# FFN-in of a hybrid conv block: product 1 of a third dual among the first products, and other pools for some of its banks

## The chip, the cores and the metric

One core of a Trainium2 chip runs the whole kernel. The metric is the time of one execution on the device in microseconds (us); the kernel before was run three times for it. Besides, one execution was profiled, and all single durations below are read from that one. TensorE (PE in the profile) does the matmuls, VectorE (DVE) and ScalarE (ACT) the elementwise work, GpSimd (POOL) some of it and part of the DMA issues, SyncE (SP) the loads of weights.

## The reference, cut to what matters

One layer of a streaming encoder: a mixing part, then a gated FFN, each behind an RMSNorm with a modulation from `c`. The change lies where the FFN begins.

```python
D_MODEL = 1024; SEQ = 1024; BATCH = 1; D_FF = 2816
...
mix = jnp.einsum('bsd,de->bse', g_a * y_a + g_b * y_b, w_o[l])
x = x + g1 * mix

h2 = rms_norm(x, norm_ffn_g[l]) * (1.0 + sc2) + sh2
a, bgate = jnp.split(jnp.einsum('bsd,df->bsf', h2, w_ffn_in[l]), 2, axis=-1)
x = x + g2 * jnp.einsum('bsf,fd->bsd', jax.nn.silu(a) * bgate, w_ffn_out[l])
...
return rms_norm(x, final_norm_g)
```

Everything is float32.

## The kernel before, in words

**Layout.** Activations lie with their channels on the 128 partitions: 8 blocks of channels by 1024 tokens, and the tokens are taken as two halves of 512, `halves[0]` and `halves[1]`. A PSUM bank holds 128 x 512 numbers, one output block for one half. A float32 operand is split into a high part, which the matmul takes as it is, and a low part, the rest: `wh` and `wl` for weights, names ending in `h` and `l` for activations. One step of a contraction is three matmuls, high by high, high by low and low by high (L283, L284, L286 in `mm3`).

**Duals.** The first matrix product of the FFN (FFN-in) has 22 blocks of 128 hidden channels, each for `a` and for `bgate`. The kernel takes two such blocks at a time, in 11 *duals*. A dual is a 2 x 2 block product: rows are `a` and `bgate`, the contraction of 1024 is two halves of 512, and columns are the two token halves. Strassen's scheme in Winograd's form does it with seven products of smaller matrices instead of eight. They are run in the order `PRODUCTS = "1265734"`. I write (d, m) for product m of dual d. One product is 24 matmuls: 2 hidden blocks (p = 0, 1), 4 contraction blocks, 3 matmuls each.

**Operands.** `ts[m]` holds the four activation pairs of product m. Products 1 and 2 need the normed `h2` of the first token half alone (pairs `h20` to `h27`). The others need combinations with the second half: t2 (product 6), t1 (5), t3 (7), b22 (3), t4 (4). So products 1 and 2 can run while the second half's norm is still being made. `norm_2_start` and `rstd_end` make `r2`, the reciprocal root of the second half's mean square (it begins at L338, with `r2t`). `norm_2_half(k, r2)` then makes h2 of the second half for channel blocks k and k + 4 (L824), and from it the t2 pair of k, whose low part is written by L323 after ScalarE's L322. `norm_2_last` makes the pairs of t1, t3, b22 and t4.

**Weights.** The left operands are sums of weight blocks. Raw blocks of 128 x 1024 numbers, 512 KB, are loaded by SyncE (L191) into five `raw` buffers. `dual_units` makes the weights of a product from them. For product 6 it adds three times (L228, L229, L230, called first, second and third sum below), for product 3 once (L232, the fourth sum); the result goes to product 6, 5, 7 or 3. `split_w` then writes `wh` on ScalarE (L205) and `wl` on VectorE (L206). Both have three buffers, and `next_w` prepares the weights two products ahead of the one about to run (`AHEAD = 2`). For a dual that is not `early`, product 1 loads all four blocks, 11, 12, 21 and 22, and the sums are in place. An `early` dual loads one block where product 1 and one where product 2 comes; the others are loaded only when products 6, 3 and 4 come, seven loads in all.

**Banks.** PSUM has eight banks: `ps` with six and `ps2` with two. A dual takes two banks of each of three kinds, for p = 0 and 1: x collects products 1, 6, 7 and 4 (each adds to what stands there), y takes product 2, z collects 5 and 3. `in_evac` reads a bank when a product of it is complete: copies for 1, 6 and 5 (L905, ScalarE), and additions on VectorE for 2 (L907), 7 (L910) and 3 (L914).

**Order.** A scheduling layer turns the program into one list of instructions for each engine, and each engine works its list in order. An instruction that waits holds all that stand behind it on its engine. The order of the products is written in `in_order`, and the weights are planned in the same order:

```python
in_order = [(d, m) for d in range(2) for m in "12"] + [(d, m) for d in range(2) for m in PRODUCTS[2:]]
in_order += [(d, m) for d in range(2, N_IN) for m in PRODUCTS]
```

So it begins (0,1), (0,2), (1,1), (1,2), then products 6, 5, 7, 3, 4 of duals 0 and 1. Ahead of it runs the last of the mixing part, `mix(j, h)`: it adds each block's result to `x` (L811), squares it on ScalarE and sums the squares (L819). The calls of `norm_2_half` stand between the first products. All this work for the second token half is on VectorE and ScalarE in the same 60 us in which TensorE runs the first products.

Of the kernel before, what the change touches and what calls it, by code (L numbers as in the profile page):

```python
# [91 lines left out]

PRODUCTS = "1265734"

GROUP, GROUPS = 3, 3
# [10 lines left out]
def block_kernel(ctx: ExitStack, tc: tile.TileContext, x0, xT, c, vecs, ada, w_first, w_plain, w_duals,  # L108
# [29 lines left out]
    def ps_tile(name):  # L138
        return psp.tile([P, H], F32, tag="ps", name=name)
# [4 lines left out]
    def hl_tile(name, dt=F32R):  # L144
        return tp.tile([P, H], dt, tag="t", name=name)
# [38 lines left out]
    def raw_tile(n=1024):  # L184

        raws.append(raws.pop(0))
        return raws[-1].tile([P, 1024], F32, tag="raw", name="raw")[:, :n]

    def load(src, n=1024):
        raw = raw_tile(n)  # L190
        nc.sync.dma_start(raw, src)  # L191
        return raw
# [6 lines left out]
    def split_w(raw, n, after=(), lo_engine=nc.vector):  # L199
        wh = whp.tile([P, 1024], F32R, tag="wh", name="wh")[:, :n]  # L200
        wl = wlp.tile([P, 1024], F32R, tag="wl", name="wl")[:, :n]
        with ExitStack() as order:
            for ins in after:
                order.enter_context(tc.issue_after(ins))
            nc.scalar.copy(wh, raw)  # L205
            lo = lo_engine.tensor_tensor(wl, raw, f32(wh), ALU.subtract)  # L206
        if n == T and lo_engine is nc.gpsimd:
            pool_los.append(lo.ins)
        return wh, wl

    def dual_units(mats, n, early=False, eng=nc.vector):

        a = {}

        def get(*blocks):
            for b in blocks:
                a[b] = load(mats[("11", "12", "21", "22").index(b)], n)

        def unit(m):
            if early:  # L220
                get(*{"1": ("11",), "2": ("12",), "6": ("21", "22", "11"), "3": ("12",), "4": ("22",)}.get(m, ()))
            elif m == "1":
                get("11", "12", "21", "22")
            if m in "12":
                return split_w(a["1" + m], n, (), eng)
            if m == "6":
                a["s1"] = a["22"] if early else raw_tile(n)
                eng.tensor_tensor(a["s1"], a["21"], a["22"], ALU.add)  # L228
                eng.tensor_tensor(a["21"], a["21"], a["11"], ALU.add)  # L229
                eng.tensor_tensor(a["11"], a["11"], a["s1"], ALU.add)  # L230
            elif m == "3":
                eng.tensor_tensor(a["12"], a["12"], a["11"], ALU.add)  # L232
            return split_w(a[{"6": "11", "5": "s1", "7": "21", "3": "12", "4": "22"}[m]], n, (), eng)

        return {m: (lambda m=m: unit(m)) for m in PRODUCTS}
# [11 lines left out]
    def next_w(ahead=AHEAD):  # L247

        fetch(ahead + 1)
        return ready.pop(0)  # L250
# [24 lines left out]
    def mm3(outs, wsl, w, xs, first, last, again=False):  # L275

        if w[1] is None:
            for ps, x in zip(outs, xs):
                mm3.ins = nc.tensor.matmul(ps, w[0][:, wsl], x, start=first, stop=last).ins
            return  # L280
        wh, wl = w[0][:, wsl], w[1][:, wsl]
        for ps, (xh, xl) in zip(outs, xs):
            nc.tensor.matmul(ps, wh, xh, start=first, stop=False, skip_group_check=again)  # L283
            nc.tensor.matmul(ps, wh, xl, start=False, stop=False, skip_group_check=again)  # L284
        for ps, (xh, _) in zip(outs, xs):
            mm3.ins = nc.tensor.matmul(ps, wl, xh, start=False, stop=last, skip_group_check=again).ins  # L286
# [5 lines left out]
            mm3(outs, slice(k * P, k * P + P), w, [act[k][h] for h in hs], k == 0, k == KC - 1)  # L292
        return outs

    def product(banks, m, t, evac=None, between=None, y_tile=ps2_tile):

        w = next_w()
        b = {"1": "x", "6": "x", "7": "x", "4": "x", "2": "y", "5": "z", "3": "z"}[m]
        n = len(t)
        for p in range(2):  # L300
            if m in "125":
                banks[b, p] = (y_tile if b == "y" else ps_tile)(b)
            ps = banks[b, p]
            for k in range(n):
                c0 = (p * n + k) * P
                mm3([ps], slice(c0, c0 + P), w, [t[k]], m in "125" and k == 0, k == n - 1, m in "6734")
            if evac:
                evac(p, m, ps)
            if between and p == 0:
                between()  # L310
# [7 lines left out]
    def t_pair(name):  # L318
        return hl_tile(name + "h"), hl_tile(name + "l")

    def t_split(src, hi, lo):
        nc.scalar.copy(hi, src)  # L322
        nc.vector.tensor_tensor(lo, src, f32(hi), ALU.subtract)  # L323

    def minus(out, a, b):

        nc.vector.scalar_tensor_tensor(out=out, in0=a, scalar=-1.0, in1=b, op0=ALU.mult, op1=ALU.subtract)
# [60 lines left out]
    x = {}  # L388
# [22 lines left out]
    def uc_tile(name, n=T + CK - 1, dt=F32):  # L411
        return ucp.tile([P, T + CK - 1], dt, tag="uc", name=name)[:, :n]
# [24 lines left out]
    for k in range(0, KC, 2):  # L437
        t = uc_tile("x0", T)
# [62 lines left out]
    KH = KC // 2  # L501
# [228 lines left out]
    banks = [[ps_tile(b) for _ in range(2)] for b in "xyz"]  # L730
# [90 lines left out]
    def h2_of(k, h, r2, hi_lo=None):  # L821

        t = x1[k][:, halves[h]]
        nc.vector.scalar_tensor_tensor(out=t, in0=t, scalar=aff2[:, k : k + 1], in1=r2, op0=ALU.mult, op1=ALU.mult)  # L824
        if hi_lo:
            hi, lo = hi_lo
            nc.scalar.activation(hi, t, AF.Identity, bias=modc(24 + k))
            nc.vector.scalar_tensor_tensor(
                out=lo, in0=t, scalar=modc(24 + k), in1=f32(hi), op0=ALU.add, op1=ALU.subtract
            )  # L830
        nc.scalar.activation(t, t, AF.Identity, bias=modc(24 + k))
        return t


    ts = {m: [None] * (KC // 2) for m in PRODUCTS}
# [9 lines left out]
    def norm_2_half(k, r2):  # L845

        h2_of(k, 1, r2)
        b22 = h2_of(k + KH, 1, r2)
        b11, b12 = (x1[k][:, s] for s in halves)
        nc.vector.tensor_tensor(b11, b11, b12, ALU.subtract)  # L850
        t2.append(hl_tile("t2", dt=F32))
        minus(t2[k], b11, b22)
        ts["6"][k] = t_pair("t2")
        t_split(t2[k], *ts["6"][k])
# [29 lines left out]


    N_IN = FC // 2
    in_units = [dual_units([w_fi[d, m] for m in range(4)], 1024, d < 2) for d in range(N_IN)]
    in_order = [(d, m) for d in range(2) for m in "12"] + [(d, m) for d in range(2) for m in PRODUCTS[2:]]
    in_order += [(d, m) for d in range(2, N_IN) for m in PRODUCTS]
    plan += [in_units[d][m] for d, m in in_order]  # L890
    ha = {}
    in_banks = [{} for _ in range(N_IN)]
# [7 lines left out]
    def in_evac(d):  # L900
        def evac(p, m, ps):
            f = 2 * d + p
            if m in "165":
                ha[f, m] = t = in_tile(d, m)
                nc.scalar.copy(t, ps)  # L905
            elif m == "2":
                nc.vector.tensor_tensor(ha[f, "1"], ps, ha[f, "1"], ALU.add)  # L907
            elif m == "7":
                t = ha[f, "5"]
                nc.vector.tensor_tensor(t, ps, t, ALU.add)  # L910
                nc.scalar.activation(t, t, AF.Silu, scale=-1.0)
            elif m == "3":
                t = ha[f, "6"]
                nc.vector.tensor_tensor(t, ps, t, ALU.add)  # L914
                nc.vector.tensor_tensor(t, t, ha[f, "5"], ALU.mult)
            else:
                t = gip.tile([P, H], F32, tag="g", name="g4")
                nc.scalar.activation(t, ps, AF.Silu, scale=-1.0)
                nc.vector.tensor_tensor(t, t, ha[f, "1"], ALU.mult)
                ha[f, "4"] = t  # L920
        return evac
# [39 lines left out]
    def group_load(g, m):  # L961
        to[g, m] = [t_load((g * GROUP + i, m)) for i in range(GROUP)]

    def in_product(d, m):
        product(in_banks[d], m, ts[m], in_evac(d), y_tile=ps_tile if d == 1 else ps2_tile)
        if d == N_IN - 1:
            group_load(0, m)

# [4 lines left out]
    r2 = None  # L973
    product(in_banks[0], "1", ts["1"], in_evac(0), norm_2_start)
    r2 = rstd_end(*r2)
    for i, (d, m) in enumerate(in_order[1:4]):
        norm_2_half(i, r2)
        in_product(d, m)
    norm_2_half(KH - 1, r2)
    norm_2_last()  # L980
    close(*phase_1)
    raws.append(open_pool("raw_a", 1, side="right", stack=ctx)[1])
    x1ap = open_pool("x1a", 2, side="right", stack=ctx)[1]
    phase_2 = [open_pool("gi", 7), open_pool("stage", 3, side="right")]
    gip, stagep = (p for _, p in phase_2)
    for d, m in in_order[4:]:
        in_product(d, m)
        if m == PRODUCTS[-1]:
            if 2 <= d < 6:
                for i in range(40 + 2 * (d - 2), 42 + 2 * (d - 2)):  # L990
                    modulation(i, x1ap.tile([P, T], F32, tag="x1", name="ada"))
            hid_set(d)
# [31 lines left out]
    for g in range(GROUPS):  # L1024
        for d in range(2):
            banks = {}
# [177 lines left out]
```

## Time and profile before

| | us |
|---|---|
| runs | 1502.62, 1504.49, 1505.2 (median 1504.49) |
| profiled execution, own time | 1502.96 |
| its span (first to last instruction) | 1501.2 |
| mean granted TensorE clock | 0.995 of full |
| loads of `in_w_fi` (weights of the FFN's first product) | 50 of 512 KB, 4.3 us from issue to landing in the median |

A row of the timeline has its start in the span, the time of one instruction, the engine, the line, the operation and its tiles; where the engine stood idle before it, the idle time and what ended it follow in brackets. A row of waits has the engine, line and tile that waited, the engine and tile that released it, the idle time, how often, and the longest. A window row gives each engine's busy time and number of instructions in a stretch, the clock granted to TensorE in it (PEclk), and the share of DMA bandwidth.

### The profile page before, as it was taken

To read this page: it belongs to the slowest core of one execution; us is meant where nothing else is said; L and a number is where in the kernel's file an instruction comes from. 1 tells how busy PE (TensorE), PEld (TensorE's weight loads), DVE (VectorE), ACT (ScalarE), POOL (GpSimd) and SP (SyncE) were. 2 spreads that over 40 slices of the span, in tenths; PEclk is the share of its full clock that TensorE was granted. 3 is DMA by queue.
4 is the path that set the end of the run, shared out by engine and by line. 5 is a ranking of instruction groups with operands and counts; after the bars stand their busy time and mean duration, and the time that the engine had idled before them with its cause. 6 is when DMAs were issued, how large, how long until landed. Compare 5 with 4: busy or idle time off the path is not lost.

```text
span 1501.2 us, 17711 instructions
## 1 busy us (share of the span) xinstructions
PE 1469.3 (98%) x6455; PEld 1202.0 (80%) x6455; DVE 1141.0 (76%) x1569; ACT 623.1 (42%) x896; POOL 538.2 (36%) x467
## 2 busy tenths in 40 slices
PE   6999999999999999999999989999999999999997
PEld 2788888888888788887788868888888888888887
DVE  7994999887887984777767789776666665667755
ACT  4653433443343353244345454444444443222235
POOL 0037777777767773410121001111000016444005
PEclk9999999999999999999999989999999999999999
DMA  9522223232222268555765337544444449998403
GB/s 352 207 64 74 94 71 112 70 108 75 98 71 85 99 261 299 167 175 175 231 207 183 126 98 236 200 169 153 152 149 150 153 148 351 364 324 256 141 28 112
DMA packets 82697, 247.24 MB, mean 165 GB/s; under 512 B 9521, under 2 KB 11697, under 8 KB 82610
## 3 DMA queue, kind: packets, MB, share of 16 engines
q1 hardware_dynamic: 41776, 137.91, 27.4%
q0 software_dynamic: 36944, 95.44, 19.2%
q10 hardware_dynamic: 3890, 12.78, 2.2%
q8 instruction: 50, 0.82, 0.2%
q14 instruction: 37, 0.30, 0.1%
HBM read 183.69 MB, written 62.39 MB: 164 GB/s over the span
## 4 chain that ended last, share of the span: by engine, by line
PE 93%; DVE 4%; issue 1%; ACT 1%; DMA 1%; POOL 0%; POOLq 0%; ACTq 0%; DVEq 0%
PE x L286 11%; PE x L284 11%; PE x L283 10%; PE z L283 7%; PE z L284 7%; PE z L286 7%; PE y L284 6%; PE y L283 6%; PE y L286 6%; PE ya L284 2%; PE mix L286 2%; PE mix L284 2%; PE ya L283 2%; PE ya L286 2%; PE mix L283 2%; PE yb L283 2%
## 5 line engine op out<-in xcount | busy, mean ns | idle before, releaser
L205 ACT CAST wh<-raw 128x1024 fp32r<-128x1024 f32 (+2 forms) x257 | 259.4, 1010 | 482.8 <-PE z L284 122.0
L206 POOL TENSOR_TENSOR wl<-raw,wh 128x1024 fp32r<-128x1024 f32 x92 | 227.2, 2471 | 131.1 <-ACT wh L205 130.9
L206 DVE TENSOR_TENSOR wl<-raw,wh 128x1024 fp32r<-128x1024 f32 (+2 forms) x165 | 188.4, 1142 | 52.7 <-ACT wh L205 50.0
L671 DVE SCALAR_TENSOR_TENSOR c<-diff,vec,c 128x512 f32<-128x512 f32 x248 | 178.6, 751 | 3.3
L930 POOL DMA_DIRECT2D hid<-stage x71 | 37.9, 534 | 358.7 <-DVE stage L323 353.0
L283 PE MATMUL x<-th,wh 128*128 128x512 f32 x240 | 93.4, 389 | 0.0
L284 PE MATMUL x<-tl,wh 128*128 128x512 f32 x240 | 93.4, 389 | 0.0
L286 PE MATMUL x<-th,wl 128*128 128x512 f32 x240 | 93.4, 389 | 0.0
L671 DVE SCALAR_TENSOR_TENSOR c<-u,wsum,c 128x512 f32<-128x512 f32 x112 | 84.1, 751 | 1.8
L264 DVE CUSTOM_DVE_ANT_0 raw<-raw,cs,vec 128x1024 f32<-128x1024 f32 x24 | 35.5, 1486 | 50.6 <-DMA raw<-in_ada 50.6
L283 PE MATMUL z<-th,wh 128*128 128x512 f32 x168 | 65.4, 389 | 0.0
L284 PE MATMUL z<-tl,wh 128*128 128x512 f32 x168 | 65.4, 389 | 0.0
L286 PE MATMUL z<-th,wl 128*128 128x512 f32 x168 | 65.4, 389 | 0.0
L228 POOL TENSOR_TENSOR raw<-raw 128x1024 f32<-128x1024 f32 x12 | 29.8, 2482 | 95.0 <-DVE wl L206 94.2
L322 ACT CAST stage<-g 128x512 fp32r<-128x512 f32 x62 | 38.3, 621 | 52.0 <-DMA hid<-stage 25.1
L323 DVE TENSOR_TENSOR stage<-g,stage 128x512 fp32r<-128x512 f32 x62 | 42.5, 688 | 20.5 <-ACT stage L322 20.4
L956 POOL DMA_DIRECT2D th<-hid x71 | 38.1, 537 | 52.0 <-PE x L286 28.3
L283 PE MATMUL yb<-zsh,wh 128*128 128x512 f32 x128 | 50.0, 391 | 2.8 <-DVE gb L793 2.8
L283 PE MATMUL x<-t2h,wh 128*128 128x512 f32 x120 | 47.7, 400 | 5.1 <-ACT wh L205 2.8
L286 PEld LDWEIGHTS x<-th,wl 128*128 128x128 f32 x240 | 45.1, 188 | 9.4
L283 PEld LDWEIGHTS x<-th,wh 128*128 128x128 f32 x240 | 45.1, 188 | 9.3
L284 PEld LDWEIGHTS x<-tl,wh 128*128 128x128 f32 x240 | 45.1, 188 | 9.3
(1012 smaller groups left out, 4263.8 us busy)
## 6 DMA issues: line engine op xcount, KB each, us to landing
hid<-stage POOLq DMA_DIRECT2D x71, 512.0 KB, 4.0
raw<-in_w_fi SPq DMA_DIRECT2D x50, 512.0 KB, 4.3
raw<-in_w_duals SPq DMA_DIRECT2D x48, 512.0 KB, 3.5
th<-hid POOLq DMA_DIRECT2D x71, 256.0 KB, 5.9
tl<-hid POOLq DMA_DIRECT2D x71, 256.0 KB, 6.0
ada<-in_ada SPq DMA_DIRECT2D x24, 512.0 KB, 5.8
raw<-in_ada SPq DMA_DIRECT2D x24, 512.0 KB, 4.5
raw<-in_w_fo SPq DMA_DIRECT2D x24, 384.0 KB, 6.2
```

The source lines that it names most:

```text
L205: nc.scalar.copy(wh, raw)
L206: lo = lo_engine.tensor_tensor(wl, raw, f32(wh), ALU.subtract)
L228: eng.tensor_tensor(a["s1"], a["21"], a["22"], ALU.add)
L264: nc.vector.tensor_tensor_reduce(out=raw, in0=raw, in1=cs, scale=1.0, scalar=col(V_ADA, b), op0=ALU.mult, op1=ALU.add, accum_out=modc(b),)
L283: nc.tensor.matmul(ps, wh, xh, start=first, stop=False, skip_group_check=again)
L284: nc.tensor.matmul(ps, wh, xl, start=False, stop=False, skip_group_check=again)
L286: mm3.ins = nc.tensor.matmul(ps, wl, xh, start=False, stop=last, skip_group_check=again).ins
L322: nc.scalar.copy(hi, src)
L323: nc.vector.tensor_tensor(lo, src, f32(hi), ALU.subtract)
L671: tap.ins = nc.vector.scalar_tensor_tensor(out=out, in0=src[:, s : s + H], scalar=wt, in1=acc, op0=ALU.mult, op1=ALU.add).ins
L930: nc.gpsimd.dma_start(hid_dram[key], s)
L956: nc.gpsimd.dma_start(t, hid_dram[key][:, s])
```

## The change

It sets `FRONT = 3`: the first products are now (0,1), (0,2), (1,1), (1,2) and (2,1). After them the order is as it was: products 6, 5, 7, 3 and 4 of duals 0 and 1, then the rest of dual 2. Dual 2 becomes `early`, so it loads seven blocks instead of four. The banks of (2,1) are not read when it is done, but right before (2,2), by the same copies (L905). So that banks suffice, other pools give them: y of dual 1 comes from `ps2` (before from `ps`), and z of dual 0 from `ps2` (before from `ps`). The call of `norm_2_half` for the last blocks now stands before (2,1), inside the loop.

```diff
+FRONT = 3
...
-    def product(banks, m, t, evac=None, between=None, y_tile=ps2_tile):
+    def product(banks, m, t, evac=None, between=None, y_tile=ps2_tile, z_tile=ps_tile):
...
             if m in "125":
-                banks[b, p] = (y_tile if b == "y" else ps_tile)(b)
+                banks[b, p] = {"x": ps_tile, "y": y_tile, "z": z_tile}[b](b)
...
-    in_units = [dual_units([w_fi[d, m] for m in range(4)], 1024, d < 2) for d in range(N_IN)]
-    in_order = [(d, m) for d in range(2) for m in "12"] + [(d, m) for d in range(2) for m in PRODUCTS[2:]]
-    in_order += [(d, m) for d in range(2, N_IN) for m in PRODUCTS]
+    in_units = [dual_units([w_fi[d, m] for m in range(4)], 1024, d < FRONT) for d in range(N_IN)]
+    in_order = [(d, m) for d in range(FRONT) for m in "12"][: 2 * FRONT - 1]
+    in_order += [(d, m) for d in range(N_IN) for m in PRODUCTS if (d, m) not in in_order]
...
     def in_product(d, m):
-        product(in_banks[d], m, ts[m], in_evac(d), y_tile=ps_tile if d == 1 else ps2_tile)
+        product(in_banks[d], m, ts[m], in_evac(d) if (d, m) != (FRONT - 1, "1") else None,
+                z_tile=ps2_tile if d == 0 else ps_tile)
...
-    for i, (d, m) in enumerate(in_order[1:4]):
+    for i, (d, m) in enumerate(in_order[1 : 2 * FRONT - 1]):
         norm_2_half(i, r2)
         in_product(d, m)
-    norm_2_half(KH - 1, r2)
     norm_2_last()
...
-    for d, m in in_order[4:]:
+    for d, m in in_order[2 * FRONT - 1 :]:
+        if (d, m) == (FRONT - 1, "2"):
+            for p in range(2):
+                in_evac(d)(p, "1", in_banks[d]["x", p])
         in_product(d, m)
```

In the changed file these lines stand three higher in number: L206 is L209 there, L228 is L231, L283 is L286, and so on.

Below are pieces of the engines' lists; the number at the end of a name tells one tile from another. The first is of TensorE, where product (1,2) ends (bank y) and (0,6) begins (operands t2, added to bank x_6496). Before:

```order
L286 MATMUL y_6662<-h27h_6223,wl_6548 128x512
L283 MATMUL x_6496<-t2h_6541,wh_6599 128x512
L284 MATMUL x_6496<-t2l_6542,wh_6599 128x512
L286 MATMUL x_6496<-t2h_6541,wl_6600 128x512
L283 MATMUL x_6496<-t2h_6586,wh_6599 128x512
```

With the change, the first rows and, 24 rows further, the last:

```order
L289 MATMUL y_6664<-h27h_6223,wl_6548 128x512
L286 MATMUL x_6693<-h20h_6181,wh_6592 128x512
L287 MATMUL x_6693<-h20l_6182,wh_6592 128x512
L289 MATMUL x_6693<-h20h_6181,wl_6593 128x512
...
L286 MATMUL x_6496<-t2h_6541,wh_6646 128x512
L287 MATMUL x_6496<-t2l_6542,wh_6646 128x512
L289 MATMUL x_6496<-t2h_6541,wl_6647 128x512
```

Product (2,1), with the h2 pairs of the first half and two banks of its own, stands between (1,2) and (0,6).

The second is VectorE's list at the end of the mixing part, up to the beginning of `r2`. Before:

```order
L228 TENSOR_TENSOR raw<-raw 128x1024
L811 SCALAR_TENSOR_TENSOR x_6084<-mix_6416,mod,xr 128x512
L206 TENSOR_TENSOR wl<-raw,wh 128x1024
L819 TENSOR_TENSOR xr<-xr 128x512
L811 SCALAR_TENSOR_TENSOR x_6122<-mix_6447,mod,xr 128x512
L206 TENSOR_TENSOR wl<-raw,wh 128x1024
L819 TENSOR_TENSOR xr<-xr 128x512
L229 TENSOR_TENSOR raw<-raw 128x1024
L230 TENSOR_TENSOR raw<-raw 128x1024
L232 TENSOR_TENSOR raw<-raw 128x1024
L338 SCALAR_TENSOR_TENSOR r2t<-r2r 128x512
```

With the change:

```order
L814 SCALAR_TENSOR_TENSOR x_6084<-mix_6416,mod,xr 128x512
L209 TENSOR_TENSOR wl<-raw,wh 128x1024
L822 TENSOR_TENSOR xr<-xr 128x512
L231 TENSOR_TENSOR raw<-raw 128x1024
L814 SCALAR_TENSOR_TENSOR x_6122<-mix_6447,mod,xr 128x512
L209 TENSOR_TENSOR wl<-raw,wh 128x1024
L822 TENSOR_TENSOR xr<-xr 128x512
L232 TENSOR_TENSOR raw<-raw 128x1024
L233 TENSOR_TENSOR raw<-raw 128x1024
L341 SCALAR_TENSOR_TENSOR r2t<-r2r 128x512
```

The first sum of dual 0 (L228 before, L231 now) has moved behind the first of these mixing rows, and the fourth (L232 before) is gone from here.

The third is VectorE's list further on, among the splits of t3 and b22, where the three sums of dual 1 stand. Before:

```order
L206 TENSOR_TENSOR wl<-raw,wh 128x1024
L323 TENSOR_TENSOR t3l<-x_5932,t3h 128x512
L228 TENSOR_TENSOR raw<-raw 128x1024
L323 TENSOR_TENSOR t3l<-x_5970,t3h 128x512
L229 TENSOR_TENSOR raw<-raw 128x1024
L323 TENSOR_TENSOR b22l<-x_6008,b22h 128x512
L230 TENSOR_TENSOR raw<-raw 128x1024
L323 TENSOR_TENSOR b22l<-x_6046,b22h 128x512
```

With the change:

```order
L235 TENSOR_TENSOR raw<-raw 128x1024
L326 TENSOR_TENSOR t3l<-x_5932,t3h 128x512
L326 TENSOR_TENSOR t3l<-x_5970,t3h 128x512
L209 TENSOR_TENSOR wl<-raw,wh 128x1024
L326 TENSOR_TENSOR b22l<-x_6008,b22h 128x512
L209 TENSOR_TENSOR wl<-raw,wh 128x1024
L326 TENSOR_TENSOR b22l<-x_6046,b22h 128x512
L231 TENSOR_TENSOR raw<-raw 128x1024
L326 TENSOR_TENSOR b22l<-x_6084,b22h 128x512
L232 TENSOR_TENSOR raw<-raw 128x1024
L326 TENSOR_TENSOR b22l<-x_6122,b22h 128x512
L233 TENSOR_TENSOR raw<-raw 128x1024
```

The fourth sum of dual 0 (L235 now) and all four splits of b22 stand ahead of dual 1's third sum, where before one split of b22 did.

## The prediction, as it was put on record

> **What bounds the kernel now.** I read the page first (busy time and the line of the clock), then TensorE's waits, then the two stretches that they pointed to.
>
> ```profile
> span 1501.2 us, 17711 instructions
> PE 1469.3 (98%) x6455; PEld 1202.0 (80%) x6455; DVE 1141.0 (76%) x1569; ACT 623.1 (42%) x896; POOL 538.2 (36%) x467
> PE x L283 <- ACT wh L205: 2.8, 1, 2.8
> PE x L283 <- ACT t2h L322: 2.3, 1, 2.3
> PE x L286 <- DVE wl L206: 1.0, 1, 1.0
> ```
>
> TensorE is busy 98% of the span. The last three rows are all that it waits for between 840 and 1490 us, and they lie in the stretch that the change rearranges. From there on an engine other than TensorE sets nothing, so what the change is worth is decided between 840 and 900 us. TensorE's own rows there:
>
> ```profile
> 853.19 0.39 PE L283 MATMUL x<-h20h,wh 128*128 128x512 f32 x1
> 855.91 0.39 PE L283 MATMUL x<-h20h,wh 128*128 128x512 f32 x1
> 864.07 0.39 PE L283 MATMUL x<-t2h,wh 128*128 128x512 f32 x1
> 870.83 0.73 PE L283 MATMUL x<-t2h,wh 128*128 128x512 f32 x2 [2.28 <-ACT t2h L322]
> 885.36 0.40 PE L286 MATMUL x<-t3h,wl 128*128 128x512 f32 x1
> 888.57 0.50 PE L283 MATMUL x<-t2h,wh 128*128 128x512 f32 x1 [2.81 <-ACT wh L205]
> 890.89 0.79 PE L286 MATMUL x<-t2h,wl 128*128 128x512 f32 x1 [1.03 <-DVE wl L206]
> 896.73 0.39 PE L283 MATMUL z<-b22h,wh 128*128 128x512 f32 x1
> ```
>
> Twelve matmuls go by from 853.19 to 855.91: 0.227 us each, 24 for a product, so 5.44 us. From 864.07, where (0,6) begins, to 896.73 stand three products and 18 matmuls of (1,6), 90 in all: 20.4 us of work in 32.7 us, so **12.3 us are lost** here. 6.1 us of that are the three bracketed waits. Most of the rest is the clock:
>
> ```profile
> core 0: us, PE busy (x) PEld busy (x) DVE busy (x) ACT busy (x) POOL busy (x), PEclk, DMA share, GB/s
> 870.00:875.00 5.00, 4.05 (x11) 2.87 (x12) 5.00 (x10) 3.53 (x7) 0.00 (x0) 0.75 0.00 2
> 875.00:880.00 5.00, 5.00 (x21) 4.10 (x21) 4.83 (x7) 2.49 (x5) 0.00 (x0) 0.91 0.16 23
> 885.00:890.00 5.00, 2.05 (x8) 0.94 (x6) 5.00 (x7) 2.53 (x5) 0.00 (x0) 0.95 0.11 43
> 890.00:895.00 5.00, 4.11 (x10) 3.23 (x11) 5.00 (x8) 3.88 (x7) 0.00 (x0) 0.50 0.37 113
> 895.00:900.00 5.00, 5.00 (x21) 4.07 (x20) 0.39 (x2) 0.71 (x2) 0.00 (x0) 0.87 0.53 202
> ```
>
> Each row of 5 us costs 5 times what its granted clock lacks: 1.25 + 0.45 us after the first wait (1.7), 0.25 + 2.5 + 0.65 after the second and third (3.4), together 5.1. The remaining 1.1 us are tenths between matmuls that wait for operands. The same rows name the bound: **VectorE is busy 4.8 to 5.0 of 5 us** until 895. TensorE's two gaps are VectorE being late, once with the last t2 pair and once with the sum of weights ahead of (1,6).
>
> **The change part by part.** VectorE's list is walked with the rows of before; in the changed file its lines stand 3 lower, and I use the old numbers.
>
> ```profile
> 841.46 0.75 DVE L811 SCALAR_TENSOR_TENSOR x<-mix,mod,xr 128x512 f32<-128x512 f32 x1 [1.58 <-PE mix L286]
> 842.36 1.23 DVE L206 TENSOR_TENSOR wl<-raw,wh 128x1024 fp32r<-128x1024 f32 x1
> 847.14 1.23 DVE L232 TENSOR_TENSOR raw<-raw 128x1024 f32<-128x1024 f32 x1 [0.56 <-DMA raw<-in_w_fi]
> 848.28 0.68 DVE L338 SCALAR_TENSOR_TENSOR r2t<-r2r 128x512 f32<-128x512 f32 x1
> 852.19 1.41 DVE L824 SCALAR_TENSOR_TENSOR x<-x,aff,r2r 128x512 f32<-128x512 f32 x2
> 857.39 1.22 DVE L206 TENSOR_TENSOR wl<-raw,wh 128x1024 fp32r<-128x1024 f32 x1
> 858.52 0.69 DVE L323 TENSOR_TENSOR t2l<-t,t2h 128x512 fp32r<-128x512 f32 x1
> 859.12 0.68 DVE L327 SCALAR_TENSOR_TENSOR t<-x,x 128x512 f32<-128x512 f32 x1
> 865.70 0.69 DVE L323 TENSOR_TENSOR t2l<-t,t2h 128x512 fp32r<-128x512 f32 x1 [0.42 <-ACT t2h L322]
> 871.25 0.68 DVE L323 TENSOR_TENSOR t2l<-t,t2h 128x512 fp32r<-128x512 f32 x1
> 886.14 1.22 DVE L230 TENSOR_TENSOR raw<-raw 128x1024 f32<-128x1024 f32 x1
> DMA to landing us min/median/max: 3.4/4.4/4.7
> ```
>
> From start to start a 1024-wide instruction takes 1.13 us (857.39 to 858.52) and a 512-wide one 0.60 (858.52 to 859.12).
>
> *Moved: product (2,1) ahead of (0,6).* 24 matmuls, 5.44 us, run on operands that are long there; its weights cost VectorE one more 1.13 us ahead of (0,6). (0,6) then begins at 864.07 + 5.44 = 869.5.
>
> *Moved with it: loads and sums.* The load for (2,1) takes one of five raw buffers, so each later load waits for the buffer of one product later. The first sum (L228), which stood ahead of the mixing tail, now stands ahead of L811 at 841.46, and needs a load that starts when the weights of (0,2) are split. The last landings were 3.4 to 4.7 us; that split ended near 838.1 to 839.3, so the load lands near 841.8, about when L811 could run. L811 then follows a 1.13 us sum instead of going first: 842.9, +1.5. The weights of (1,1) follow at 843.6 instead of 842.36, and their buffer's load ends as much later: the next sum starts at 848.4 instead of 847.14. Here before had one sum left to do, the change has two, so L338 starts at 848.4 + 2.26 = 850.6, **2.3 us later**. A read of a y bank (L907) is also moved ahead: L824, the start of h2's second half, goes from 852.19 to 855.0. The statistics matmul between (0,1) and (0,2) is held by the late L811 too: about 0.3 us of TensorE.
>
> *From there to the last t2 pair.* 852.19 to 871.25 is 19.06 us. The changed list has one more 1.13 us split and two 0.60 us instructions fewer, so the same length, or 0.4 less where the wait at 865.70 falls away: t2l starts at 873.7 and ends at 874.4. TensorE needs it at the 20th matmul of (0,6): 869.8 + 19 x 0.227 = 874.1. **The first wait shrinks from 2.28 us to some 0.3 us, with its cold spell of 1.7.** Behind it TensorE and VectorE run level: (0,6), (0,5), (0,7) are 72 matmuls, so 869.8 + 16.3 + 0.4 of small waits = 886.5.
>
> *The second wait.* (1,6) needs the third sum (L230), which waits in VectorE's list. Before, 14 short and 5 wide instructions lie from the last t2l to it (14 x 0.60 + 5 x 1.13 = 14.1, in the rows 871.25 to 886.14, 14.9 with its waits). Now the fourth sum of dual 0 (L232, done at 847.14 before) and three more splits of b22 stand there: 18 short and 6 wide, 17.6 us. The third sum starts at 873.7 + 17.6 = 891.3, 5.2 us later. Before, TensorE started 888.57 - 886.14 = 2.43 us after it, which is the sum, then
>
> ```profile
> 887.47 1.05 ACT L205 CAST wh<-raw 128x1024 fp32r<-128x1024 f32 x1 [3.98 <-DVE raw L230]
> ```
>
> so now at 893.7. **The idle time here grows from 2.81 us to 893.7 - 886.5 = 7.2 us.** (0,3) stands behind (1,6) in TensorE's list and cannot fill it. The third wait stays near 1.0: wl of (1,6) comes two t4 splits and one sum after the third sum, at 894.7, done 895.9.
>
> *Clock.* One restart instead of two. The rows bound its price from 1.7 (after 2.28 us of idling) to 3.4 us (after 2.81 and 1.03); the shape, a wait and a second wait, is that of the second, but the second wait begins sooner after the restart, so I take 2.4. The Trainium skill ("TensorE: Matmul & The Clock Gate", "HAM oscillation — how this bites in real kernels") warns of TensorE gaps over about 3.4 us. By that, the old gaps of 2.28 and 2.81 us would have cost no clock and only the new one would: 11.4 lost against 12.3 - 5.1 = 7.2, so 4.2 us slower, 1508.7. The granted clock of 0.75 and 0.50 behind the old gaps says otherwise, so this has little of my belief.
>
> *Costed at nothing.* The three extra loads (SyncE, 512 KB each) run where the DMA engines are 0 to 37% busy; if one were late, it would add to VectorE's lateness (below). The y banks of dual 1 now wait for L907 of dual 0, which runs near 853 to 855, while TensorE gets there at 858.6: 3 us of cover. The two x banks of dual 2 stay full until (2,2), and z of dual 1 takes those of dual 0, free 1.2 us after (0,4), while 17 matmuls of (1,6) (3.9 us) run in between. TensorE's list from (2,2) on is unchanged.
>
> **Sum.** Lost now: 7.2 + 1.0 + 2.4 + 0.3 + 0.3 + 0.2 = 11.4 us against 12.3: 0.9 us less. The profiled execution took 1502.96 us (1.8 around its span), so 1502.1; the median of the runs is 1.5 higher at 1504.49, so **1503.6 us**. What a measurement can tell from no change is about 0.2%, 3.0 us: I forecast no difference.
>
> **Rivals.** *Faster: the long wait costs no clock* and the third wait vanishes behind it. Lost 11.4 - 2.4 - 1.0 = 8.0, so 4.3 us gained: 1500.2. For it, the clock stands at 0.95 from 885 to 890, so it closes only near the end of a wait; against it, both restarts in the rows are cold. Chance 0.18 with all cases over 3 us. That VectorE's early lateness does not come (loads landing before L811) gives less than it seems: ScalarE's list now has the copy of (1,1)'s first bank, which ends near 856, ahead of the x14 step that VectorE waits for, so of 2.8 us about 1.4 stay; 1502.2, counted within 0.2%.
>
> *Slower: the two loads in series.* The first sum waits for one load, the next sum for another that starts only after it. At 4.7 us each instead of 3.5, L338 is 2.4 us later still, and as the t2 pair has no slack, all of it opens the first wait again. Beyond about 2 us of idling the cold spell returns (1.7): 11.4 + 2.4 + 1.7 = 15.5, 3.2 us over before, 1507.7. For it: L232 already waits 0.56 us for such a load. Against: the landing at 847.14 took 3.55 us after the split ended. Chance 0.18, with other losses.
>
> **How the numbers follow.** Forecast and all cases within 3.0 us: 0.64. Faster 0.18, slower 0.18. The forecast's own range, with the cold spell between 1.7 and 3.4 and the landings between 3.4 and 4.4, is 1502.3 to 1506. Reaching to both rivals, since the chances outside it are open-ended: 1500.2 to 1507.7.
>
> **What would show it.** Right: no wait over 1 us for t2h; (0,6) starting near 869.8; one wait of 6.5 to 8 us before (1,6) for wh, released through the third sum near 891 on VectorE; clock below 1 only after it, in one spell of 3 to 7 us; L338 near 850.6; no TensorE wait after 900. Wrong: a t2h wait over 2 us (loads late), a wh wait under 5 us (VectorE's list less full than counted), a wait at the y or z banks, or a wait in later duals from the changed turn of the raw buffers.

## The result, and the profile after

| | before | changed |
|---|---|---|
| median of 19 runs each, us | 1504.35 (1501.14 to 1507.2) | 1506.85 (1505.18 to 1508.76) |
| profiled execution, own time | 1502.96 | 1507.61 |
| its span | 1501.2 | 1505.8 |

The ratio is 1.0019 with a 95% interval of 1.0012 to 1.0026: the change costs 2.5 us. The prediction was a gain of 0.9 us.

The page of the changed kernel has TensorE busy for the same time in a longer span, and what it waits for between 840 and 1490 us is this (engine, line and tile that waits, what released it, us in total, times, longest):

```profile
span 1505.8 us, 17717 instructions
PE 1468.6 (98%) x6455; PEld 1200.9 (80%) x6455; DVE 1141.0 (76%) x1569; ACT 623.8 (41%) x896; POOL 538.2 (36%) x467
PE x L286 <- ACT wh L208: 7.0, 1, 7.0
PE x L286 <- DVE g L913: 1.6, 1, 1.6
PE x L289 <- DVE wl L209: 0.9, 2, 0.6
PE x L286 <- ACT g L908: 0.7, 1, 0.7
PE ss L407 <- DVE xr L822: 0.3, 1, 0.3
```

The two waits near 870 and 888 have become one of 7.0 us, and three have come that were not there: for L913, for L908 and for one L209. TensorE's timeline puts them in place (start in the span, time of one, and in brackets the idle time before it):

```profile
842.79 0.39 PE L286 MATMUL x<-h20h,wh 128*128 128x512 f32 x1
871.46 0.39 PE L286 MATMUL x<-t2h,wh 128*128 128x512 f32 x1
895.13 0.79 PE L286 MATMUL x<-t2h,wh 128*128 128x512 f32 x1 [6.98 <-ACT wh L208]
914.94 0.39 PE L286 MATMUL z<-t1h,wh 128*128 128x512 f32 x1
933.02 0.50 PE L286 MATMUL x<-t4h,wh 128*128 128x512 f32 x1 [1.59 <-DVE g L913]
944.04 0.39 PE L286 MATMUL x<-t2h,wh 128*128 128x512 f32 x1
955.73 0.50 PE L286 MATMUL x<-t3h,wh 128*128 128x512 f32 x1 [0.66 <-ACT g L908]
957.11 0.50 PE L289 MATMUL x<-t3h,wl 128*128 128x512 f32 x1 [0.65 <-DVE wl L209]
983.99 0.39 PE L286 MATMUL x<-t2h,wh 128*128 128x512 f32 x1
```

These rows are, from the top: the start of (0,1), of (0,6), of (1,6) after its wait, of (1,5), of (1,4) after its wait, of (2,6), two waits in (2,7), the start of (3,6). In the kernel before the same starts are these:

```profile
841.26 0.39 PE L283 MATMUL x<-h20h,wh 128*128 128x512 f32 x1
908.97 0.39 PE L283 MATMUL z<-t1h,wh 128*128 128x512 f32 x1
941.61 0.39 PE L283 MATMUL x<-t2h,wh 128*128 128x512 f32 x1
979.69 0.39 PE L283 MATMUL x<-t2h,wh 128*128 128x512 f32 x1
```

From start to start, less 5.44 us for each product that lies between, is what TensorE loses in a stage:

| stage | before | changed |
|---|---|---|
| (0,1) to (0,6): 4 products before, 5 now | 1.05 | 1.47 |
| (0,6) to (1,5): 6 products | 12.3 | 10.8 |
| (1,5) to (2,6): 6 before, 5 now | 0.0 | 1.9 |
| (2,6) to (3,6): 7 products | 0.0 | 1.9 |
| sum, (0,1) to (3,6): 23 products, 125.1 us | 13.3 | 16.1 |

So the stages that the prediction worked out, the first two rows, gained 1.0 us against its 0.9, and **3.8 us were lost behind them**, where the prediction expected nothing. From (3,6) to the last group of matmuls both take 511.36 us. The profiled executions differ by 4.6 us and not by 2.8 because the changed one came to (0,1) 1.5 us later and ended 0.3 us later behind the last matmuls. Over the runs below that start lies between 841.3 and 843.0 without the moved product and between 842.2 and 844.9 with it. Below the sum of the table is compared, not the span; a loss of a part of a microsecond ahead of (0,1) is not excluded by it.

Behind the new waits stand VectorE and ScalarE:

```profile
924.57 0.69 DVE L326 TENSOR_TENSOR stage<-g,stage 128x512 fp32r<-128x512 f32 x1 [1.95 <-ACT stage L325]
929.93 0.69 DVE L326 TENSOR_TENSOR stage<-g,stage 128x512 fp32r<-128x512 f32 x1 [3.19 <-ACT stage L325]
932.28 0.68 DVE L913 TENSOR_TENSOR g<-x,g 128x512 f32<-128x512 f32 x1
```

```profile
923.91 0.62 ACT L325 CAST stage<-g 128x512 fp32r<-128x512 f32 x1 [3.81 <-DMA hid<-stage]
929.28 0.62 ACT L325 CAST stage<-g 128x512 fp32r<-128x512 f32 x1 [3.31 <-DMA hid<-stage]
954.58 0.62 ACT L325 CAST stage<-g 128x512 fp32r<-128x512 f32 x1 [2.17 <-DMA hid<-stage]
```

The results of dual 0 are split into `stage` buffers and stored, seven times. There are three such buffers, so from the fourth split on, each waits until an earlier store has landed. L913 reads the bank of (1,7), which (1,4) then adds to. It had to wait for nothing itself: (1,7)'s first half ended near 923.1 (its start at 920.4 and half of 5.44). It stood in VectorE's list behind splits that waited for stores. The two waits in (2,7) have the same form: L908 at 955.10 stands behind the cast of 954.58, and the `wl` split of (2,7) (L209, 955.84) behind a split that started at 955.23, after 1.50 us of waiting for its cast.

For the first of these waits the lists differ from those of before. VectorE's list from the fourth split on, before, with the two reads of (1,7)'s banks (L910) behind the fifth and the sixth split:

```
L323 TENSOR_TENSOR stage<-g_6933,stage 128x512
L206 TENSOR_TENSOR wl<-raw,wh 128x1024 x2
L323 TENSOR_TENSOR stage<-g_6789,stage 128x512
L910 TENSOR_TENSOR g_7043<-x,g_7043 128x512
L228 TENSOR_TENSOR raw<-raw 128x1024
L323 TENSOR_TENSOR stage<-g_6803,stage 128x512
L910 TENSOR_TENSOR g_7058<-x,g_7058 128x512
L206 TENSOR_TENSOR wl<-raw,wh 128x1024
L323 TENSOR_TENSOR stage<-g_6948,stage 128x512
```

With the change, where all seven splits stand ahead of the first read (now L913):

```
L326 TENSOR_TENSOR stage<-g_6965,stage 128x512
L209 TENSOR_TENSOR wl<-raw,wh 128x1024
L231 TENSOR_TENSOR raw<-raw 128x1024
L326 TENSOR_TENSOR stage<-g_6821,stage 128x512
L209 TENSOR_TENSOR wl<-raw,wh 128x1024
L326 TENSOR_TENSOR stage<-g_6835,stage 128x512
L232 TENSOR_TENSOR raw<-raw 128x1024
L326 TENSOR_TENSOR stage<-g_6980,stage 128x512
L913 TENSOR_TENSOR g_7075<-x,g_7075 128x512
```

### The profile page after: what moved, and what is told of

Same layout as the page of the kernel before. It is cut to its first block, busy times and chain, and to the rows that moved or that the text cites. A ratio compares the mean times of both kernels' runs of the same rounds, so it can differ in the third digit from the quotient of the medians.

```text
span 1505.8 us, 17717 instructions
## 1 busy us (share of the span) xinstructions
PE 1468.6 (98%) x6455; PEld 1200.9 (80%) x6455; DVE 1141.0 (76%) x1569; ACT 623.8 (41%) x896; POOL 538.2 (36%) x467
## 4 chain that ended last, share of the span: by engine, by line
PE 78%; issue 14%; DVE 3%; POOL 2%; DMA 2%; ACT 1%; POOLq 0%; SPq 0%; DVEq 0%; ACTq 0%
PE x L289 9%; PE x L286 9%; PE x L287 9%; PE z L286 6%; PE z L287 6%; PE z L289 6%; PE y L286 6%; PE y L287 5%; PE y L289 5%; PE ya L286 2%; PE ya L289 2%; PE ya L287 2%; PE lead L282 1%; PE lead L286 1%; PE lead L289 1%
## 5 line engine op out<-in xcount | busy, mean ns | idle before, releaser
L209 POOL TENSOR_TENSOR wl<-raw,wh 128x1024 fp32r<-128x1024 f32 x92 | 227.5, 2474 | 131.0 <-ACT wh L208 124.2
L209 DVE TENSOR_TENSOR wl<-raw,wh 128x1024 fp32r<-128x1024 f32 (+2 forms) x165 | 188.4, 1143 | 64.7 <-ACT wh L208 62.1
L286 PE MATMUL x<-th,wh 128*128 128x512 f32 x240 | 93.4, 389 | 0.0
L286 PE MATMUL z<-th,wh 128*128 128x512 f32 x168 | 65.4, 389 | 0.0
L231 POOL TENSOR_TENSOR raw<-raw 128x1024 f32<-128x1024 f32 x12 | 29.8, 2485 | 96.1 <-DVE wl L209 95.3
L286 PE MATMUL x<-t2h,wh 128*128 128x512 f32 x120 | 47.6, 397 | 7.0 <-ACT wh L208 7.0
L286 PE MATMUL yb<-zsh,wh 128*128 128x512 f32 x128 | 50.0, 391 | 3.3 <-DVE gb L796 3.3
L286 PEld LDWEIGHTS x<-th,wh 128*128 128x128 f32 x240 | 45.1, 188 | 9.2
```

## The experiments

Each kernel was timed beside the kernel before on the same chip (before's medians: 1503.99, 1504.12 and 1504.8 us in the three groups). "Lost" is the sum of the table above, (0,1) to (3,6), in the profiled execution. It is the figure of one execution: before and pools_only, which keeps the lists of before, have 13.3 and 11.8.

| run | us, median | ratio to before (95%) | lost, us |
|---|---|---|---|
| pools_only | 1504.04 | 1.0003 (0.9994 to 1.0012) | 11.8 |
| five_loads | 1504.79 | 1.0002 (0.9993 to 1.0011) | 13.5 |
| set_later | 1503.03 | 0.9994 (0.9985 to 1.0002) | 11.9 |
| gp_sums_after | 1508.95 | 1.0033 (1.0022 to 1.0045) | 16.8 |
| o3_set_later | 1505.18 | 1.0007 (0.9998 to 1.0016) | 12.8 |
| o3_before | 1506.34 | 1.0012 (1.0003 to 1.0021) | 14.7 |
| set_later_before | 1503.76 | 1.0000 (0.9991 to 1.0009) | 13.5 |
| o3_after | 1505.38 | 1.0006 (0.9997 to 1.0015) | 13.6 |
| early3_before | 1504.16 | 0.9997 (0.9988 to 1.0006) | 12.6 |
| zt_set_later | 1496.30 | 0.9946 (0.9934 to 0.9959) | 6.0 |
| zb_set_later | 1497.16 | 0.9954 (0.9942 to 0.9967) | 5.6 |
| zb_before | 1500.62 | 0.9977 (0.9968 to 0.9987) | 7.8 |

### What makes the loss after 900 us

**pools_only**: the change without its product order and early loads.

```diff
-FRONT = 3
+FRONT = 2
...
-    in_order = [(d, m) for d in range(FRONT) for m in "12"][: 2 * FRONT - 1]
+    in_order = [(d, m) for d in range(FRONT) for m in "12"]
```

> The product order and the loads of before, with only the bank kinds of the change (y of dual 1 and z of dual 0 both from the pool of two banks). The lists of all engines stand as before. Theory A (the change's loss comes from the moved product: one product of TensorE's cover is taken from the stretch after 900 us and spent before 870): this costs nothing, 1504.4 within 1 us, the two waits near 870 and 888 as before, none over 0.3 us after 900. Theory B (the bank kinds cost something): slower by 1 us or more, with a wait for a y or z bank.

No wait for a bank, and no time. The bank kinds cost nothing.

**five_loads**: dual 2 loads 21, 22 and a second 11 with product 2 and keeps 12, as later duals do.

```diff
-    in_units = [dual_units([w_fi[d, m] for m in range(4)], 1024, d < FRONT) for d in range(N_IN)]
+    in_units = [dual_units([w_fi[d, m] for m in range(4)], 1024, d < FRONT - 1 or (2 if d == FRONT - 1 else False)) for d in range(N_IN)]
```

> The change, but dual 2 loads five blocks instead of seven (one for product 1, four for product 2, the sums in place as in later duals). Theory C (the extra loads share the DMA engines with the stores of the hidden blocks and make these late): the waits of 1.6, 0.7 and 0.7 us between 930 and 960 fall to under 0.5 in sum, and the kernel runs near 1504. Theory A (lost cover): they stay between 2 and 4 us in sum, 1506 to 1507.5. The wait of 7 us before (1,6) stays in both.

The three waits are gone; one of 0.56 us came in (2,4). That looked like theory C. But VectorE's list differs too: the first read of (1,7)'s bank stands ahead of the seventh split instead of behind all seven. So this run alone does not tell loads from list.

**set_later**: the same work of dual 0, called after (1,7).

```diff
-            hid_set(d)
+            if d:
+                hid_set(d)
+        if (d, m) == (1, "7"):
+            hid_set(0)
```

> The change, but the work that splits and stores dual 0's hidden blocks is written behind product (1,7) in the program, so that the reads of the x banks after (1,7) stand ahead of five of the seven splits in VectorE's list instead of behind all. Theory A with the list as its means (reads of banks queue behind splits that wait for stores): the wait of 1.6 us before (1,4) falls under 0.3; the two of 0.7 us in (2,7) stay or grow a little, since the stores of duals 0 and 1 lie closer together: 1505 to 1506. Theory C (loads): all three waits stay, since the loads do not change: 1506.9.

TensorE has no wait in this list after 900 us, though the seven loads of dual 2 are all there, and from (1,5) to (3,6) it loses 0.4 us instead of 3.8:

```profile
PE x L286 <- ACT wh L208: 7.0, 1, 7.0
PE ss L407 <- DVE xr L822: 0.4, 1, 0.4
PE x L289 <- DVE wl L209: 0.3, 1, 0.3
```

It takes 3.8 us off the change's 1506.85 us, as much as the table lost behind (1,5). The expectation that (2,7) would still wait was wrong, and this says something about those two waits. In set_later L908 and the `wl` split for (2,7) stand behind the same cast and the same split as in the change, yet TensorE does not wait: L908 runs at 953.00, 9.6 us after (2,6) starts, and in the change 11.1 us after. Dual 1's first split is also earlier, 0.9 us ahead of the start of (2,6) (942.48) instead of 0.6 us behind it (944.64). So for (2,7) the order alone does not make the wait. That dual 1's work came later because the L913 reads did is argued from the rows, not tested by itself.

**set_later_before**: the same edit in the kernel before.

> The kernel before with the stores of dual 0 written behind (1,7) as in set_later. If set_later repaired a loss of the change: no wait to remove here, 1504 within 1 us. If writing the stores later is a gain by itself: 1 us or more faster, 1503 or less.

No gain. So set_later repairs a loss that the change made, and is no gain of its own.

**early3_before**: the loads alone.

```diff
-    in_units = [dual_units([w_fi[d, m] for m in range(4)], 1024, d < 2) for d in range(N_IN)]
+    in_units = [dual_units([w_fi[d, m] for m in range(4)], 1024, d < 3) for d in range(N_IN)]
```

> The kernel before with dual 2 loading seven blocks instead of four, one by one as its products come; the lists of TensorE, VectorE, ScalarE and GpSimd are those of before. Theory C (the extra loads by themselves make the stores of hidden blocks late and so the bank reads): stores of dual 0 land up to 8 or 9 us after issue, and a wait of 1 us or more appears before (1,4) or (2,7): 1505.5 to 1507. Theory F (the order of VectorE's list is needed too: in the list of before the read of (1,7)'s bank stands behind one split that has to wait for a store, in the change's behind three): no wait over 0.5 us after 900, 1504 within 1 us.

Between 905 and 935 us the stores land like this, first in the kernel before, then with the early loads, then in the change (min, median, max):

```profile
DMA to landing us min/median/max: 2.9/4.3/7.1
```

```profile
DMA to landing us min/median/max: 3.1/6.4/9.9
```

```profile
DMA to landing us min/median/max: 3.0/6.1/9.1
```

The early loads do make the stores late, as late as in the change. But TensorE waits for nothing after 900 us. In this list the first read of (1,7)'s bank (L910, 921.50) stands ahead of the split that is held longest. The second read stands behind that split:

```profile
920.89 0.69 DVE L323 TENSOR_TENSOR stage<-g,stage 128x512 fp32r<-128x512 f32 x1 [1.75 <-ACT stage L322]
921.50 0.68 DVE L910 TENSOR_TENSOR g<-x,g 128x512 f32<-128x512 f32 x1
922.10 1.21 DVE L228 TENSOR_TENSOR raw<-raw 128x1024 f32<-128x1024 f32 x1
925.97 0.69 DVE L323 TENSOR_TENSOR stage<-g,stage 128x512 fp32r<-128x512 f32 x1 [2.66 <-ACT stage L322]
926.58 0.68 DVE L910 TENSOR_TENSOR g<-x,g 128x512 f32<-128x512 f32 x1
```

(1,4) starts at 925.58 here and comes to its second bank at 928.30, so the second read, done at 927.26, is 1.0 us early. Theory F's forecast came true: the late stores cost nothing with the list of before. Their cost depends on how many held splits stand ahead of a bank read, and on how soon TensorE needs that bank. Theory A, that a product of cover was lost, fell already with set_later, which has no more cover than the change.

### What the wait of 7 us is made of

**gp_sums_after**: dual 1's sums on GpSimd.

```diff
-                eng.tensor_tensor(a["s1"], a["21"], a["22"], ALU.add)
+                sums.tensor_tensor(a["s1"], a["21"], a["22"], ALU.add)
...
-    in_units = [dual_units([w_fi[d, m] for m in range(4)], 1024, d < FRONT) for d in range(N_IN)]
+    in_units = [dual_units([w_fi[d, m] for m in range(4)], 1024, d < FRONT, sums=nc.gpsimd if d == 1 else None) for d in range(N_IN)]
```

> The change, but the four sums of weights of dual 1 are made on GpSimd, which has nothing to do between 845 and 905 us. If the wait of 7 us before (1,6) is VectorE's queue ahead of the third sum (18 short and 6 wide instructions), it falls under 1.5 us and the cold clock behind it goes: 7 to 9 us less, 1498 to 1500. If something else is late for (1,6) at the same time (its loads or the wh cast), 3 us or more of the wait stay: 1502 to 1504. The waits after 930 stay, or grow to 4 us, as TensorE comes there earlier.

The first branch failed. Of the second the wait held, not the time: the wait did not shrink but grew to 8.2 us, and the kernel is 2 us slower than the change. Of the waits after 930 us one of 0.55 us is left, which the expectation did not have either. GpSimd's first sum, and VectorE beside it:

```profile
887.23 2.60 POOL L233 TENSOR_TENSOR raw<-raw 128x1024 f32<-128x1024 f32 x1 [40.54 <-DMA raw<-in_w_fi]
```

```profile
886.36 1.23 DVE L209 TENSOR_TENSOR wl<-raw,wh 128x1024 fp32r<-128x1024 f32 x1
887.50 2.87 DVE L328 TENSOR_TENSOR b22l<-x,b22h 128x512 fp32r<-128x512 f32 x1
890.30 3.36 DVE L209 TENSOR_TENSOR wl<-raw,wh 128x1024 fp32r<-128x1024 f32 x1
```

The sums could not start before 887.23, since their last raw block landed only then: its buffer is freed by the split for (0,7). GpSimd then took 8.6 us for the three sums, to 895.85. And beside GpSimd's sums, VectorE's instructions took 2.87 and 3.36 us instead of 0.69 and 1.22.

**o3_after, o3_set_later, o3_before**: (1,6) may not stand ahead of (0,3) in TensorE's list.

```diff
+    after = {}
+
     def in_product(d, m):
+        with ExitStack() as order:
+            if (d, m) in after:
+                order.enter_context(tc.issue_after(after[d, m]))
+            in_product_of(d, m)
+        if (d, m) == (0, "3"):
+            after[1, "6"] = mm3.ins
+
+    def in_product_of(d, m):
```

> The change with the rule for TensorE's list alone, stores as in the change. Theory D: 5 us less than the change in the stretch up to (1,5), and the waits of 1.6 and 2 x 0.7 us after it stay (stores ahead of bank reads in the lists): 1501 to 1503, 2 to 4 us above o3_set_later. Theory E: 1506 to 1507.

> The run set_later, and besides (1,6) may not stand ahead of (0,3) in TensorE's list, so that the order there is (0,7), (0,3), (0,4), (1,6). In the trace of the change TensorE is idle from 888 to 895 us with (1,6) at the head of its list, while the last b22 split of (0,3) ends at 892.8 and its weights at 888.7. Theory D (the wait is the order of TensorE's list: what it waits for is the only thing not ready): (0,3) starts near 888 and is held by the b22 splits until 893, (0,4) by the t4 splits until 899, (1,6) by nothing; about 3 to 4 us of waits instead of 7, a shorter cold spell, (1,5) some 5 us earlier: 1497 to 1500. Theory E (VectorE is the bound here whatever the order): what is saved before (1,6) comes back as waits of the same sum in (0,3) and (0,4): 1502 to 1504.

> The kernel before with the same rule for TensorE's list ((1,6) not ahead of (0,3)). Theory D: the waits of 2.8 and 1.0 us before (1,6) shrink to 1 to 2 us in (0,3), 1501 to 1503; less to gain than with the moved product, as the wait is shorter. Theory E: 1504.

Neither theory as worded, and the times lie outside the ranges of both in all three. There is again one wait, now before (0,3), 8.5 us in the change and 5.9 in the kernel before. In o3_set_later:

```profile
PE z L286 <- ACT g L908: 8.5, 1, 8.5
```

```profile
894.96 1.04 ACT L208 CAST wh<-raw 128x1024 fp32r<-128x1024 f32 x1 [4.25 <-DVE raw L233]
895.91 1.13 ACT L325 CAST t4h<-x 128x512 fp32r<-128x512 f32 x2
896.95 1.06 ACT L908 COPY g<-z 128x512 f32<-128x512 f32 x2
```

(0,3) adds to the z banks that (0,5) left, and they must be copied first. The copies were possible after (0,5), but stand in ScalarE's list behind the weight cast of (1,6), which waits for the third sum. So (1,6)'s lateness holds (0,3) through a third engine. o3_after kept a wait of 1.3 us for L913, so the loss after 900 us repeats in another kernel with that list.

**zt_set_later**: ScalarE's casts behind the z copies, and the sums of dual 1 behind the t4 splits.

```diff
+    def behind(d, m):
+        with ExitStack() as order:
+            if (d, m) == (1, "6"):
+                order.enter_context(tc.issue_after(t4_last[0]))
+            order.enter_context(tc.issue_after(z_copies[-1]))
+            return in_units[d][m]()
...
-    plan += [in_units[d][m] for d, m in in_order]
+    plan += [(lambda d=d, m=m: behind(d, m)) if (d, m) in ((0, "4"), (1, "6")) else in_units[d][m] for d, m in in_order]
```

> The run set_later with two rules for the lists: the weight casts of (0,4) and (1,6) on ScalarE stand behind the copies of (0,5)'s z banks (which (0,3) adds to; in o3_set_later they stood behind the cast that waits for the third sum), and the sums of dual 1 on VectorE stand behind the t4 splits. TensorE's order is then (0,7), (0,3), (0,4), (1,6). If the wait of 8.5 us in o3_set_later was ScalarE's queue: (0,3) starts about 2.7 us after (0,7) ends, (0,4) and (1,6) follow with under 1 us of waits, (1,5) starts 5 to 7 us earlier than in set_later: 1496 to 1499. If VectorE is the bound whatever the order: 1502 to 1504.

As the queue theory has it. The waits between 840 and 1490 us are down to

```profile
PE z L286 <- ACT g L919: 2.3, 1, 2.3
PE ss L407 <- DVE xr L822: 0.2, 1, 0.2
```

and the kernel takes 1496.3 us, **8.5 us less than before** and, by its median, the fastest here. The two rules were not tried one by one.

**zb_set_later, zb_before**: besides, the b22 and t4 splits are written behind (0,5).

```diff
+    for d, m in in_order[2 * FRONT - 1:2 * FRONT - 1 + 2]:
+        in_product(d, m)
+    with tc.issue_after(z_copies[-1]):
+        norm_2_rest()
```

> As zt_set_later, and the b22 and t4 splits are written behind (0,5) in the program, with their casts on ScalarE behind the copies of (0,5)'s z banks, so that these run as soon as (0,5) is done. If the queues are the cause: (0,3) starts at once after (0,7), under 2 us of waits between 870 and 910, the clock stays at 1.0 there: 8 to 10 us less than set_later, 1493 to 1496. If VectorE is the bound: 1502 to 1504.

> The kernel before (product order without (2,1) ahead) with the rules of zb_set_later, stores as before. The wait of 2.3 us for the last t2 pair stays, with 0 to 1.7 us of cold clock behind it; the waits of 2.8 and 1.0 us before (1,6) go: 5 to 7 us less than before, 1497 to 1499. So the moved product is worth 2 to 4 us once the second wait is gone; if the two come out level, the moved product gives nothing even then.

Both times lie above their ranges. zb_set_later no longer waits before (0,3), but it waits 2.4 us before (1,6): the hole moved, and the time is that of zt_set_later within a microsecond. zb_before keeps the wait of 2.3 us for t2 and one of 1.6 us before (1,6); it takes 4.2 us less than before, so about half of the gain of 8 us needs no moved product. It is 3.5 us slower than zb_set_later (of another store order, which was worth nothing in the kernel before). So the moved product is worth about 3.5 us, within the 2 to 4 that were expected, once nothing gives it back; the two intervals leave it between about 1 and 6 us.

## Why the prediction was wrong

- **(2,1) as cover, the first wait gone: right.** Said: (0,6) starts at 869.8 and the t2 wait shrinks to 0.3 us. (0,6) started at 871.46, which is 869.9 with the later start of (0,1) taken off, and no t2h wait is left.
- **VectorE's early lateness: right.** L338 (now L341) was put at 850.6; it ran 2.7 us later than before with the start taken off (852.47), at 850.9.
- **The second wait: right.** 7.2 us and a third sum at 891.3 were forecast; 6.98 us and 892.70 (891.2 with the start off) came. VectorE's list set it, with the 18 short and 6 wide instructions that were counted. What the working left out is how little lies behind that list: in gp_sums_after the last block that the first sum needs landed at 887.23, some 2.5 us ahead of the change's first sum (889.23, with a start 0.6 us apart), so the sums could not have begun more than that earlier.
- **The clock and the third wait: right in sum, by luck.** 2.4 and 1.0 us were taken, and the two errors, some 0.8 us each, cancel. The third wait was 0.25 us (0.9 for the two wl waits, less the 0.65 in (2,7)); the clock cost 3.2 us, half of the 4.87 us that TensorE ran in the first of these windows and 5 x 0.16 in the second (the granted clock is the third number from the end):

```profile
895.00:900.00 5.00, 4.62 (x10) 3.23 (x11) 4.80 (x7) 4.14 (x8) 0.00 (x0) 0.50 0.29 83
900.00:905.00 5.00, 5.00 (x20) 3.98 (x20) 1.06 (x2) 0.47 (x1) 0.00 (x0) 0.84 0.69 228
```

- **The banks: right.** No wait for a y or z bank in the change, and pools_only costs nothing.
- **What failed** is the step that left the rest out: "From there on an engine other than TensorE sets nothing, so what the change is worth is decided between 840 and 900 us", and with it "TensorE's list from (2,2) on is unchanged". TensorE's list is, but VectorE's and ScalarE's are not. The reads of (1,7)'s banks stand further behind the splits for the stores there, the work behind them comes later too, and 3.8 us were lost on it. That lies outside the forecast's own terms, and none of the rivals had it. The prediction did name a wait in later duals as a sign of being wrong, but from the turn of the raw buffers, not from the lists of VectorE and ScalarE. Without these 3.8 us its sum would have held by the table: 1.0 us gained against 0.9.
- **The extra loads** were costed at nothing because the DMA engines were 0 to 37% busy, read from windows that end at 900 us, the last of which has 53% already. In the change, loads of dual 2 started at 916.10, 921.55 and 926.77, where the engines are full. So they were before; here is the same window, first before, then with the change (the DMA share is the last number but one):

```profile
915.00:920.00 5.00, 5.00 (x24) 4.14 (x23) 3.05 (x3) 2.11 (x4) 2.21 (x5) 1.00 0.96 280
915.00:920.00 5.00, 5.00 (x24) 4.14 (x23) 4.39 (x7) 3.90 (x7) 0.80 (x2) 1.00 0.94 335
```

The difference comes after it: from 925 to 935 us the share is 0.56 and 0.00 before, 1.06 and 0.98 with the change. The cost of nothing was right by itself, as early3_before shows, though for another reason than the one given: the stores do land later, and with the list of before the reads that TensorE needs still come in time. In the change's list they do not. How much of the 3.8 us would remain with that list and without the early loads was not tried. For the wait of 1.6 us five_loads allows an estimate: its first read ran at 927.88 and not at 932.28, 2.7 us of that because the sixth split was released earlier (927.27, not 929.93), the other 1.7 us by its place in the list. Either alone would have about covered that wait.

## What to carry to other kernels

Here a moved product shifted the planner's order on other engines too, far beyond the stretch that it left. So the lists of all engines are compared up to the place where they read alike again, and each bank read and cast that TensorE needs is checked for what stands ahead of it and waits for a buffer. An instruction that was ready and stands behind one that is not is a wait that no row of the kernel before shows, and writing the waiting work later in the program can remove it: here 3.8 us for the stores, and 8.5 us against the kernel before with the z copies and the dual 1 sums put right as well. In the kernel before, where those reads came in time, the same edit gave nothing.

## What the runs showed of the hardware

**The clock after a wait of 2.3 us is not always cold.** pools_only has the lists of before and the same wait (2.27 us, for t2h), but the window behind it, and for comparison the window of zt_set_later with its wait of 2.28 us, are:

```profile
870.00:875.00 5.00, 4.02 (x16) 2.70 (x17) 5.00 (x10) 3.89 (x7) 0.00 (x0) 1.00 0.01 2
```

```profile
890.00:895.00 5.00, 5.00 (x15) 3.94 (x16) 5.00 (x8) 3.68 (x5) 0.00 (x0) 0.66 0.50 176
```

In the kernel before, the clock was 0.75 in the window of the first and 0.91 in the next; in pools_only both have 1.00. So one wait of this length cost 0 or 1.7 us here, and two executions of the same lists differed by that. The Trainium skill ("TensorE: Matmul & The Clock Gate", "HAM oscillation — how this bites in real kernels") sets the limit at gaps over about 3.4 us; here 2.3 us were enough in some executions.

**GpSimd's sums slow VectorE's.** In gp_sums_after a 128x512 split took 2.87 us and a 128x1024 one 3.36 us beside GpSimd's 2.60 us sums, 2.2 and 2.1 us more than alone. The Trainium skill ("SBUF — State Buffer", "Who interferes with whom") says that a VectorE instruction with two SBUF inputs contends with a GpSimd instruction that reads SBUF, over a shared port pair that is an exclusive lock; these rows agree with that.
